# Gate matmuls of a decoder trunk: merged [high | low] products, weight sums on another queue, loads a block ahead

## The chip, the cores and the metric

The kernel runs on one core of a Trainium2 chip. The metric is the device time of one execution in microseconds (us), as the median of three runs. Engines are called PE (TensorE), ACT (ScalarE), DVE (VectorE), POOL (GpSimd) and SP (SyncE, which here issues nearly all transfers).

## The reference

One layer of a hybrid decoder trunk for 512 tokens, D = 2048, float32. The input is normalised and modulated (h), one projection w_in gives all branches, and the gates of the two branches come from the same projection:

```
p = h @ w_in[l]
cv, cg, cz, q, k, v, az, m_conv, m_attn = jnp.split(p, offsets, axis=-1)
y_conv = (silu(layer_norm(conv(cv * sigmoid(cg)))) * silu(cz)) @ w_conv_out
y_attn = (rms_norm(diff_attention(q, k, v)) * (1 - lam_0) * silu(az)) @ w_attn_out
merged = sigmoid(m_conv) * y_conv + sigmoid(m_attn) * y_attn
x = x + gate * rms_norm(merged @ w_o[l], g_post[l])
```

(The conv and attention lines are shortened.) The change concerns the columns cz (1024 wide), m_attn and m_conv (2048 wide each) of the projection. The code's names for the two m parts are ma and mc: the 8 blocks ma and the 8 blocks mc.

## The kernel before

Every large product is made in float32 precision from pairs: a value is split into a high part (a cast, ACT, line 145) and a low part (value minus high, DVE, line 146), and mm3 (lines 165 to 171) issues three matmuls for each 128x128 piece of weights, high·high, high·low and low·high. Weights come as 1 MB pieces through wraw (line 154, three buffers, SP's queue) and are split by wsplit into 128x1024 high and low tiles (wh and wl, three buffers each).

Stages follow one another on TensorE: conv and modulation (0 to 243 us), values, queries, keys and attention heads (to 605), az (559.5 to 664.7, the silu gate of attention; groups az0 to az3 of 256 columns), then the gate stage (664.7 to 1072.5), the attention output (py_ya, to 1159.6), the conv output (py_yc, to 1247) and the last projection (pw).

The gate stage makes 20 blocks of 256 output columns: cz0 to cz3, ma0 to ma7, mc0 to mc7. Each block is one step of a two-by-two Strassen scheme with 7 products instead of 8 (gemm_blocks, line 681). A product is 8 pieces of weights times mm3 on 256 moving columns, 24 matmuls; a block has 168. The weight operands are a11, a12, a22 straight from the loaded pieces, and four sums s1 = a21 + a22, s2 = s1 + a11, s3 = a11 + a21, s4 = s2 + a12 that DVE makes (lines 705, 706, 715, 724). The moving operands are quarters of h (B11, B21, B22, T1) and sums of them (T2, T3, T4), which block_sums makes on DVE and ACT during az, a step at a time (paced). The accumulators z, x and y each take up several products, and DVE joins their intermediate states in ta and tb (lines 711 to 727). The order of the products is z (a11), x (s2), y (s1), x (s3), z (a12), x (a22), y (s4): the second product of a block needs s2.

PE's order in the stage is fixed by the order of the code (ordered). The other engines' orders follow a scheduler that places instructions by its own estimates of readiness, so an instruction can stand behind one that waits. pump advances other work (conv_stats: mean and variance of the conv branch, fetched as cv and stored as cd) by one step after each product. Finished tiles are stored to DRAM by spill (line 433, SP's queue) and read back by fetch (line 438).

The tiles of the gate stage lie in a pool (mq, line 668) that is opened where the pool of the attention stage is closed (front.close(), line 667): the first writer of such a tile waits for the users of the space that was there before.

## Time and profile before

| what | us |
|---|---|
| median of three runs (1434.76 to 1435.95) | 1435.48 |
| the profiled execution | 1436.9 |
| its span in the trace | 1435.1 |
| PE busy in the span | 1397.3 (97%) |
| DVE busy | 1080.9 (75%) |
| ACT busy | 522.1 (36%) |
| gate stage, 664.7 to 1072.5 | 407.8 |

The span is what the trace covers; some 1.8 us of the execution lie around it. PE is busy nearly throughout, so what PE does one after the other makes the time, except at the ends and where it waits.

### The profile page before, as it was taken

Reading aid. Unit: us, or ns where it says so; the run is one execution under the profiler, and the core shown is the slowest. Engines: PE = TensorE matmul, PEld = TensorE weight load, DVE = VectorE, ACT = ScalarE, POOL = GpSimd, SP = SyncE. Lnnn points to the kernel's source line nnn. Section 1 sums busy time; section 2 is a strip of 40 time slices with the busy share of each in tenths; the row PEclk is TensorE's granted clock in tenths of the full one; section 3 lists DMA queues with packets and bytes.
Section 4 is the critical chain, followed back from the end, with each engine's and each line's share of the span. In section 5 each row is a group of like instructions: output and inputs, shape, how many; then the busy total and the mean of one; then the engine's idle time right before and its main releaser. Section 6 shows DMA issues by size and latency. Waiting matters only on the chain.

```text
span 1435.1 us, 20362 instructions
## 1 busy us (share of the span) xinstructions
PE 1397.3 (97%) x7999; PEld 1189.5 (83%) x7999; DVE 1080.9 (75%) x1750; ACT 522.1 (36%) x839; POOL 1.8 (0%) x8
## 2 busy tenths in 40 slices
...
GB/s 301 288 280 304 237 123 92 125 121 59 117 67 96 103 67 84 86 111 142 224 128 192 198 170 174 172 140 121 134 233 350 280 243 181 88 107 231 190 147 147
DMA packets 178338, 238.62 MB, mean 166 GB/s; under 512 B 8689, under 2 KB 119618, under 8 KB 177346
## 3 DMA queue, kind: packets, MB, share of 16 engines
...
HBM read 210.02 MB, written 27.26 MB: 165 GB/s over the span
## 4 chain that ended last, share of the span: by engine, by line
PE 90%; DVE 5%; DMA 2%; ACT 1%; issue 1%; SPq 0%; DVEq 0%; ACTq 0%
PE pw L167 12%; PE pc L167 11%; PE py_ya L167 6%; PE py_yc L167 6%; PE pv L167 6%; PE pg_az L167 5%; PE pg_q L167 5%; PE pg_k L167 5%; PE x_ma L167 5%; PE x_mc L167 4%; PE z_ma L167 3%; PE y_ma L167 3%; PE y_mc L167 3%; PE z_mc L167 3%; PE x_cz L167 2%; PE y_cz L167 2%
## 5 line engine op out<-in xcount | busy, mean ns | idle before, releaser
L500 DVE SCALAR_TENSOR_TENSOR cacc<-u,cw,cacc 128x511 f32<-128x511 f32 (+14 forms) x240 | 164.4, 728 | 0.0
L167 PE MATMUL pc<-hp,wh_c 128*128 128x512 f32 x512 | 159.9, 397 | 3.0 <-DVE part L369 1.2
L167 PE MATMUL pw<-wh_o,mgs 128*128 128x512 f32 x448 | 140.6, 393 | 0.0
L167 PEld LDWEIGHTS pc<-hp,wh_c 128*128 128x128 f32 x512 | 95.6, 190 | 29.0 <-issue 2.7
L167 PE MATMUL pc<-hp,wl_c 128*128 128x512 f32 x256 | 99.0, 396 | 2.1 <-DVE wl_c L146 2.1
L167 PEld LDWEIGHTS pw<-wh_o,mgs 128*128 128x128 f32 x448 | 84.1, 188 | 18.9 <-ACT fsq L932 0.7
L167 PE MATMUL pw<-wl_o,mgs 128*128 128x512 f32 x224 | 87.2, 389 | 0.0
L369 DVE TENSOR_TENSOR part<-pc,part 128x512 f32<-128x512 f32 x96 | 64.7, 687 | 25.3 <-PE pc L167 25.0
L167 PE MATMUL pv<-wh_v,hp 128*128 128x512 f32 x256 | 82.8, 397 | 0.9 <-DVE part L369 0.9
L167 PE MATMUL pg_q<-hp,wh_q 128*128 128x512 f32 x256 | 82.7, 398 | 0.0
L167 PE MATMUL pg_az<-hp,wh_az 128*128 128x512 f32 x256 | 81.5, 395 | 0.0
L167 PE MATMUL pg_k<-hp,wh_k 128*128 128x512 f32 x256 | 80.1, 392 | 0.0
L167 PE MATMUL py_ya<-ya,wh_ya 128*128 128x512 f32 x256 | 78.7, 389 | 0.0
L146 DVE TENSOR_TENSOR wl_o<-wr_o,wh_o 128x1024 fp32r<-128x1024 f32 x28 | 34.2, 1222 | 52.7 <-ACT wh_o L145 52.7
L145 ACT CAST wh_c<-wr_c 128x1024 fp32r<-128x1024 f32 (+1 forms) x36 | 34.2, 955 | 104.0 <-DMA wr_c<-in_w_in_dram 54.9
L889 DVE SCALAR_TENSOR_TENSOR accg<-adag,cact,accg 128x512 f32<-128x512 f32 x60 | 45.1, 751 | 32.2 <-DMA adag<-in_w_ada_dram 31.1
L145 ACT CAST wh_o<-wr_o 128x1024 fp32r<-128x1024 f32 x28 | 29.5, 1052 | 104.5 <-PE pw L167 93.0
L167 PEld LDWEIGHTS pc<-hp,wl_c 128*128 128x128 f32 x256 | 48.5, 190 | 14.1 <-DVE wl_c L146 3.3
L167 PEld LDWEIGHTS pv<-wh_v,hp 128*128 128x128 f32 x256 | 47.8, 188 | 14.3 <-issue 4.5
L167 PEld LDWEIGHTS pg_az<-hp,wh_az 128*128 128x128 f32 x256 | 47.7, 188 | 12.0 <-issue 2.7
L167 PEld LDWEIGHTS pg_q<-hp,wh_q 128*128 128x128 f32 x256 | 47.2, 188 | 12.4 <-issue 2.8
L167 PEld LDWEIGHTS py_ya<-ya,wh_ya 128*128 128x128 f32 x256 | 48.0, 188 | 9.9
...
## 6 DMA issues: line engine op xcount, KB each, us to landing
ada<-in_w_ada_dram SPq DMA_DIRECT2D x128, 256.0 KB, 5.4
wr_ma<-in_w_in_dram SPq DMA_DIRECT2D x16, 1024.0 KB
wr_mc<-in_w_in_dram SPq DMA_DIRECT2D x16, 1024.0 KB, 5.2
adag<-in_w_ada_dram SPq DMA_DIRECT2D x32, 512.0 KB, 5.0
wr_o<-in_w_o_dram SPq DMA_DIRECT2D x16, 1024.0 KB, 5.1
wr_c<-in_w_in_dram SPq DMA_DIRECT2D x28, 512.0 KB, 6.1
wr_v<-in_w_in_dram SPq DMA_DIRECT2D x8, 1024.0 KB, 5.1
wr_q<-in_w_in_dram SPq DMA_DIRECT2D x8, 1024.0 KB, 5.0
```

Source lines behind the costliest of these rows:

```text
L145: nc.scalar.copy(hi, src)
L146: i = nc.vector.tensor_tensor(lo, src, hi.bitcast(F32), op=ALU.subtract)
L167: mm = nc.tensor.matmul(ps, a[p], b[q], start=start and i == 0, stop=stop and i == 2, skip_group_check=more)
L369: nc.vector.tensor_tensor(part[i], ps[f], part[i], op=ALU.add)
L500: paced(nc.vector.scalar_tensor_tensor(cvo[t][:, s:], u[t][:, :S - s], wj, cvo[t][:, s:], op0=ALU.mult, op1=ALU.add))
L889: nc.vector.scalar_tensor_tensor(acc, raw[:, k, :], s1, acc, op0=ALU.mult, op1=ALU.add)
```

## The change

The pair of a moving operand is kept in one tile (hp, halves_of), high part and low part side by side. Where a product is wide, the high weights multiply [high | low] as one matmul of 512 columns into a full bank, and the low weights multiply the high part (256 columns) into its first half: two matmuls instead of three. DVE adds the second half afterwards (comb, and the added lines behind the copies of z). z and y products are wide in every block, x products in mc alone.

s1 is made by two transfers on POOL's queue, a copy and an accumulating one; in mc, s3 too (an accumulating transfer into the loaded piece). Loads go a block ahead (block_load, next_load), o and az of the ma blocks too, and these are now split in place. All stores of the stage go to ACT's queue. conv_stats advances at every other product. block_sums splits T2, T3 and T4 apart, 256 columns each. Temporary tiles are 10 instead of 12, s1 has two buffers and s2 one.

```diff
 NTEMP = 14
-NTEMP2 = 12
+NTEMP2 = 10
...
+                hp[k] = pair_of(f"hp_{k}")
+                h[k] = hi, lo = hp[k][:, 0, :], hp[k][:, 1, :]
...
+    def spill(key, g, queue=nc.sync):
         scratch[key] = dram.tile([P, S], F32, name=f"scratch_{key}")
-        nc.sync.dma_start(out=scratch[key], in_=g)
+        queue.dma_start(out=scratch[key], in_=g)
...
-    T23, T4 = [None] * KH, [None] * KH
+    T2, T3, T4 = [None] * KH, [None] * KH, [None] * KH
     t1s = [temp(f"t1_{i}") for i in range(KH // 2)]
+
+    def halves_of(src, name):
+
+        g = page(name, F32R)
+        split(src, g[:, :H2], g[:, H2:], pace=True)
+        return g.rearrange("p (a n) -> p a n", a=2)
...
-            hi, lo = page(f"t23h_{k}", F32R), page(f"t23l_{k}", F32R)
-            split(t23, hi, lo, pace=True)
-            T23[k] = (hi, lo)
+            T2[k] = halves_of(t23[:, :H2], f"t2_{k}")
+            T3[k] = halves_of(t23[:, H2:], f"t3_{k}")
             yield
-            if k % 2:
-                hi, lo = page(f"t4h_{k}", F32R), page(f"t4l_{k}", F32R)
-                split(t4, hi, lo, pace=True)
-                for i in range(2):
-                    T4[k - 1 + i] = (hi[:, i * H2:(i + 1) * H2], lo[:, i * H2:(i + 1) * H2])
-                yield
+            T4[k] = halves_of(t4[:, half], f"t4_{k}")
+            yield
...
+    B11 = [g[:, :, :H2] for g in hp[:KH]]
+    T1 = [g[:, :, H2:] for g in hp[:KH]]
+    B21 = [g[:, :, :H2] for g in hp[KH:]]
+    B22 = [g[:, :, H2:] for g in hp[KH:]]
...
+    blocks, done = {}, [0]
+
+    def block_load(src, c0, name):
+
+        s1 = mp.tile([P, KH, P], F32, tag="s1", bufs=2, name=f"s1_{name}")
+        v = src.rearrange("(t p) n -> p t n", p=P)
+        nc.gpsimd.dma_start(out=s1, in_=v[:, :KH, c0 + P:c0 + 2 * P])
+        nc.gpsimd.dma_start(out=s1, in_=v[:, KH:, c0 + P:c0 + 2 * P], accum_op=ALU.add)
         r1 = wraw(src, 0, KH, c0, 256, f"{name}_1")
-        r2 = wraw(src, KH, KH, c0, 256, f"{name}_2")
-        a11, a21 = r1[:, :, :P], r1[:, :, P:]
+        if name[:2] == "mc":
+            nc.gpsimd.dma_start(out=r1[:, :, P:], in_=v[:, :KH, c0:c0 + P], accum_op=ALU.add)
+        blocks[name] = [s1, r1]
+        yield
+        blocks[name].append(wraw(src, KH, KH, c0, 256, f"{name}_2"))
...
+        s1, r1, r2 = blocks.pop(name)
+        a11, s3 = r1[:, :, :P], r1[:, :, P:]
         a12, a22 = r2[:, :, :P], r2[:, :, P:]
-
-        def tsum(i):
-            return mp.tile([P, KH, P], F32, tag="ws", bufs=2, name=f"ws_{name}_{i}")
-
-        def prod(ps, w, b, first):
+        s2 = mp.tile([P, KH, P], F32, tag="s2", bufs=1, name=f"s2_{name}")
+        xwide = name[:2] == "mc"
+
+        def prod(ps, w, b, first, wide=True):
 
             hi, lo = w
+            psv = ps.rearrange("p (a n) -> p a n", a=2)
             for k in range(KH):
-                mm3(ps[:, :H2], (hi[:, k, :], lo[:, k, :]), b[k], first and k == 0, k == KH - 1, not first, ordered)
-            pump(rate[0])
+                if wide:
+                    ordered(nc.tensor.matmul(psv, hi[:, k, :], b[k], start=first and k == 0, stop=False,
+                                             skip_group_check=True))
+                    ordered(nc.tensor.matmul(ps[:, :H2], lo[:, k, :], b[k][:, 0, :], start=False, stop=k == KH - 1,
+                                             skip_group_check=True))
+                else:
+                    mm3(ps[:, :H2], (hi[:, k, :], lo[:, k, :]), (b[k][:, 0, :], b[k][:, 1, :]), first and k == 0,
+                        k == KH - 1, not first, ordered)
+            done[0] += 1
+            if done[0] % 2:
+                pump(rate[0])
+
+        def comb(out, ps, a, op0, op1, wide=True):
+
+            nc.vector.tensor_tensor(out, ps[:, :H2], a, op=op0)
+            if wide:
+                nc.vector.tensor_tensor(out, ps[:, H2:], out, op=op1)
 
         z, xx, y = [gbank(f"{n}_{name}", tag) for n, tag in (("z", "g"), ("x", "s"), ("y", "g"))]
-        s1, s2 = tsum(1), tsum(2)
         ta, tb = temp(f"ta_{name}"), temp(f"tb_{name}")
-        q1, u2 = ta[:, :H2], ta[:, H2:]
+        q1, u2 = tb[:, :H2], ta[:, H2:]
         w11 = wsplit(a11, f"{name}_a11")
-        nc.vector.tensor_tensor(s1, a21, a22, op=ALU.add)
+        prod(z, w11, B11, True)
         nc.vector.tensor_tensor(s2, s1, a11, op=ALU.add)
-        prod(z, w11, B11, True)
         nc.scalar.copy(q1, z[:, :H2])
+        nc.vector.tensor_tensor(q1, z[:, H2:], q1, op=ALU.add)
         ws2 = wsplit(s2, f"{name}_s2")
-        prod(xx, ws2, T2, True)
+        prod(xx, ws2, T2, True, xwide)
+
         nc.vector.tensor_tensor(u2, q1, xx[:, :H2], op=ALU.subtract)
+        if xwide:
+            nc.vector.tensor_tensor(u2, u2, xx[:, H2:], op=ALU.subtract)
         ws1 = wsplit(s1, f"{name}_s1")
         prod(y, ws1, T1, True)
-        nc.vector.tensor_tensor(tb[:, H2:], q1, y[:, :H2], op=ALU.add)
-        nc.vector.tensor_tensor(a21, a11, a21, op=ALU.add)
-        ws3 = wsplit(a21, f"{name}_s3")
-        prod(xx, ws3, T3, False)
-        nc.vector.tensor_tensor(tb[:, H2:], xx[:, :H2], tb[:, H2:], op=ALU.subtract)
+        comb(tb[:, H2:], y, q1, ALU.add, ALU.add)
+        if name[:2] != "mc":
+            nc.vector.tensor_tensor(s3, a11, s3, op=ALU.add)
+        ws3 = wsplit(s3, f"{name}_s3")
+        prod(xx, ws3, T3, False, xwide)
+        next(loads[0], None)
+        comb(tb[:, H2:], xx, tb[:, H2:], ALU.subtract, ALU.add, xwide)
         w12 = wsplit(a12, f"{name}_a12")
         prod(z, w12, B21, False)
+        nc.scalar.copy(ta[:, :H2], z[:, :H2])
+        nc.vector.tensor_tensor(ta[:, :H2], z[:, H2:], ta[:, :H2], op=ALU.add)
         w22 = wsplit(a22, f"{name}_a22")
-        prod(xx, w22, T4, False)
-        nc.vector.tensor_tensor(tb[:, :H2], xx[:, :H2], q1, op=ALU.subtract)
+        prod(xx, w22, T4, False, xwide)
+        comb(q1, xx, q1, ALU.subtract, ALU.add, xwide)
         nc.vector.tensor_tensor(s2, s2, a12, op=ALU.add)
         ws4 = wsplit(s2, f"{name}_s4")
         prod(y, ws4, B22, False)
-        nc.vector.tensor_tensor(u2, u2, y[:, :H2], op=ALU.add)
-        return z, ta, tb
-
-    def silu2(i, z, ta, tb):
+        comb(u2, y, u2, ALU.add, ALU.add)
+        return ta, tb
...
+    todo = [(C_CZ + j * 256, f"cz{j}") for j in range(4)]
+    todo += [(c0 + j * 256, f"{name}{j}") for c0, name in ((C_MA, "ma"), (C_MC, "mc")) for j in range(8)]
+    todo = deque(todo)
+
+    loads = [block_load(w_in[0], *todo.popleft())]
+    for _ in range(2):
+        next(loads[0], None)
...
+    def next_load():
+
+        loads[0] = block_load(w_in[0], *todo.popleft()) if todo else iter(())
+        next(loads[0], None)
+
     for pair in range(4):
-        gs = silu2(pair, *gemm_blocks(w_in[0], C_CZ + pair * 256, f"cz{pair}"))
+        next_load()
+        gs = silu2(pair, *gemm_blocks(f"cz{pair}"))
         for f in range(2):
-            spill(f"cz{2 * pair + f}", gs[f])
+            spill(f"cz{2 * pair + f}", gs[f], nc.scalar)
     for c0, name in ((C_MA, "ma"), (C_MC, "mc")):
         for j in range(8):
-            z, ta, tb = gemm_blocks(w_in[0], c0 + j * 256, f"{name}{j}")
-            g0, g1 = temp(f"{name}0_{j}"), temp(f"{name}1_{j}")
-            nc.scalar.activation(g0[:, :H2], z[:, :H2], AF.Tanh, scale=0.5)
-            nc.scalar.activation(g0[:, H2:], ta[:, H2:], AF.Tanh, scale=0.5)
-            nc.scalar.activation(g1, tb, AF.Tanh, scale=0.5)
-            spill(f"{name}{2 * j}", g0)
-            spill(f"{name}{2 * j + 1}", g1)
+            next_load()
             if name == "ma":
                 o, az = temp(f"o_{j}"), temp(f"az_{j}")
                 fetch(f"o{j}", o)
                 fetch(f"az{j}", az)
+            ta, tb = gemm_blocks(f"{name}{j}")
+            g0, g1 = temp(f"{name}0_{j}"), temp(f"{name}1_{j}")
+            nc.scalar.activation(g0, ta, AF.Tanh, scale=0.5)
+            nc.scalar.activation(g1, tb, AF.Tanh, scale=0.5)
+            spill(f"{name}{2 * j}", g0, nc.scalar)
+            spill(f"{name}{2 * j + 1}", g1, nc.scalar)
+            if name == "ma":
                 nc.vector.tensor_tensor(o, o, az, op=ALU.mult)
-                hi, lo = temp(f"oh_{j}", F32R), temp(f"ol_{j}", F32R)
-                split(o, hi, lo)
-                spill(f"yah{j}", hi.bitcast(F32))
-                spill(f"yal{j}", lo.bitcast(F32))
+                split(o, az.bitcast(F32R), o.bitcast(F32R))
+                spill(f"yah{j}", az, nc.scalar)
+                spill(f"yal{j}", o, nc.scalar)
```

The first place is the border between az and the first gate block, on DVE. Names: wl_az, hp and t4l are splits of az weights, of t1 and of the block sums; ws_cz (after: s_cz) are weight sums, wl_cz_s their low parts. Before:

```order
L146 TENSOR_TENSOR t4l_5523<-t_6_5443,t4h_5522 128x512
L146 TENSOR_TENSOR wl_az_12_5551<-wr_az_8_5510,wh_az_12_5550 128x1024
L146 TENSOR_TENSOR wl_cz_a_5624<-wr_cz_1_5612,wh_cz_a_5623 128x1024
L705 TENSOR_TENSOR ws_cz_1_5619<-wr_cz_1_5612,wr_cz_2_5614 128x1024
L706 TENSOR_TENSOR ws_cz_2_5620<-ws_cz_1_5619,wr_cz_1_5612 128x1024
L715 TENSOR_TENSOR wr_cz_1_5612<-wr_cz_1_5612 128x8x128
L146 TENSOR_TENSOR wl_cz_s_5657<-ws_cz_2_5620,wh_cz_s_5656 128x1024
L724 TENSOR_TENSOR ws_cz_2_5620<-ws_cz_2_5620,wr_cz_2_5614 128x1024
```

After, from the last block sum's split (t, 128x256):

```order
L146 TENSOR_TENSOR t_7_5575<-t_6_5489,t_7_5575 128x256
L748 TENSOR_TENSOR wr_cz_1_5646<-wr_cz_1_5646 128x8x128
L658 SCALAR_TENSOR_TENSOR sz_5618<-sz_5618,pg_az_0_5432 128x512
L658 SCALAR_TENSOR_TENSOR sz_5623<-sz_5623,pg_az_1_5433 128x512
L737 TENSOR_TENSOR tb_cz_5653<-z_cz_5649,tb_cz_5653 128x256
L735 TENSOR_TENSOR s_cz_5648<-s_cz_5636,wr_cz_1_5639 128x1024
L146 TENSOR_TENSOR wl_cz_s_5680<-s_cz_5648,wh_cz_s_5679 128x1024
L146 TENSOR_TENSOR wl_cz_s_5709<-s_cz_5636,wh_cz_s_5708 128x1024
L146 TENSOR_TENSOR wl_cz_s_5732<-wr_cz_1_5639,wh_cz_s_5731 128x1024
```

The last split of block sums stood ahead of the az and cz splits and three rows ahead of the first weight sum; now those splits come earlier, and it is the last one before the gate stage's own work. s2 (L735) stands behind a sum for the next block (L748), the two sz and the first add on z (L737), and DVE no longer makes s1.

POOL issues s1's transfers in this order (L687 the copy, L688 the accumulating one), where before it issued none:

```order
L687 DMA s_cz_5636<-in_w_in_dram 128x8x128
L687 DMA s_cz_5643<-in_w_in_dram 128x8x128
L688 DMA s_cz_5636<-in_w_in_dram 128x8x128
L688 DMA s_cz_5643<-in_w_in_dram 128x8x128
L687 DMA s_cz_5846<-in_w_in_dram 128x8x128
L688 DMA s_cz_5846<-in_w_in_dram 128x8x128
```

The copies of the first two blocks go out together, then their second halves; from there each block's pair follows the other.

The second place is the end of the stage on SP's queue, around the second weights of the attention output (the wr_ya row here). Before:

```order
L155 DMA wr_ya_10376<-in_w_attn_out_dram 128x8x256
L435 DMA scratch_mc_10122<-mc_6_10116 128x512
L435 DMA scratch_mc_10120<-mc_6_10115 128x512
L883 DMA adag_0_11085<-in_w_ada_dram 128x2x512
L155 DMA wr_ya_10469<-in_w_attn_out_dram 128x8x256
L438 DMA ya_10350<-scratch_yah_6865 128x512
L438 DMA ya_10350<-scratch_yal_6867 128x512
```

After:

```order
L438 DMA ya_9667<-scratch_yal_8228 128x512
L438 DMA mg_9730<-scratch_ma_6706 128x512
L438 DMA mg_9730<-scratch_ma_6708 128x512
L438 DMA cd_9745<-scratch_cd_6582 128x512
L438 DMA cd_9747<-scratch_cd_6696 128x512
L438 DMA cd_9749<-scratch_cd_6837 128x512
L438 DMA tz_9751<-scratch_cz_5842 128x512
L155 DMA wr_ya_9765<-in_w_attn_out_dram 128x8x256
L438 DMA mg_9823<-scratch_ma_6923 128x512
```

The second wr_ya went from ahead of all fetches of ya (16) to behind them, behind the first mg pair, the last three cd and the first tz.

The third place is DVE right behind that, at the low parts of these weights (wl_ya) and the addition of the first attention output (mg). Before:

```order
L727 TENSOR_TENSOR ta_mc_10133<-ta_mc_10133,y_mc_10130 128x256
L146 TENSOR_TENSOR wl_ya_0_10472<-wr_ya_10469,wh_ya_0_10471 128x1024
L146 TENSOR_TENSOR wl_ya_4_10500<-wr_ya_10469,wh_ya_4_10499 128x1024
L851 TENSOR_TENSOR cd_10443<-cd_10443,crs 128x512
L851 TENSOR_TENSOR cd_10445<-cd_10445,crs 128x512
L851 TENSOR_TENSOR cd_10447<-cd_10447,crs 128x512
L851 TENSOR_TENSOR cd_10449<-cd_10449,crs 128x512
L851 TENSOR_TENSOR cd_10451<-cd_10451,crs 128x512
L905 SCALAR_TENSOR_TENSOR mg_10434<-mg_10434,py_ya_0_10374 128x512
L905 SCALAR_TENSOR_TENSOR mg_10434<-mg_10434,py_ya_1_10375 128x512
```

After:

```order
L898 TENSOR_TENSOR cd_9749<-cd_9749,crs 128x512
L903 SCALAR_TENSOR_TENSOR cd_9735<-cth_9752,cd_9735 128x512
L905 TENSOR_TENSOR cd_9735<-cd_9735,tz_9751 128x512
L151 SCALAR_TENSOR_TENSOR ycl_9760<-cd_9735,ych_9759 128x512
L952 SCALAR_TENSOR_TENSOR mg_9730<-mg_9730,py_ya_0_9670 128x512
L146 TENSOR_TENSOR wl_ya_0_9768<-wr_ya_9765,wh_ya_0_9767 128x1024
L952 SCALAR_TENSOR_TENSOR mg_9730<-mg_9730,py_ya_1_9671 128x512
L146 TENSOR_TENSOR wl_ya_4_9796<-wr_ya_9765,wh_ya_4_9795 128x1024
```

The two low parts stood ahead of the two mg additions, with sums of cd between; now each stands behind one of them.

## Rows read from the trace of the kernel before

**Rows 1.** Gate stage: length, busy us by engine, PEclk, DMA share, GB/s.

```profile
664.70:747.00 82.30, 82.30 (x683) 81.82 (x682) 73.92 (x105) 40.50 (x54) 0.00 (x0) 1.00 0.53 180
747.00:909.80 162.80, 162.47 (x1354) 162.28 (x1354) 131.18 (x149) 74.93 (x96) 0.00 (x0) 1.00 0.55 181
909.80:1072.50 162.70, 161.57 (x1347) 161.39 (x1346) 117.89 (x127) 71.29 (x89) 0.00 (x0) 1.00 0.46 155
```

**Rows 2.** Waits of TensorE in the gate stage: us in total, times, longest.

```profile
PE x_mc L167 <- DVE tb_mc L718: 1.1, 1, 1.1
```

**Rows 3.** Timeline, TensorE, end of az, first block: start, us, operation.

```profile
664.01 0.62 PE L167 MATMUL pg_az<-hp,wh_az 128*128 128x512 f32 x2
...
664.69 0.40 PE L167 MATMUL z_cz<-hp,wh_cz_a 128*128 128x256 f32 x2
...
667.56 1.02 PE L750 MATMUL pmean<-csum,ones 128*128 128x512 f32 x2
668.02 0.68 PE L167 MATMUL x_cz<-t23h,wh_cz_s 128*128 128x256 f32 x1
```

**Rows 4.** VectorE and ScalarE groups, gate stage: busy us, mean ns, idle.

```profile
L705 DVE TENSOR_TENSOR ws_ma<-wr_ma,wr_ma 128x1024 f32<-128x1024 f32 x8 | 9.8, 1220 | 0.3 <-DMA wr_ma<-in_w_in_dram 0.3
...
L723 DVE TENSOR_TENSOR tb_ma<-x_ma,ta_ma 128x256 f32<-128x256 f32 x8 | 3.4, 424 | 1.5 <-PE x_ma L167 1.3
...
L145 ACT CAST wh_ma_s<-ws_ma 128x1024 fp32r<-128x1024 f32 x24 | 25.2, 1050 | 37.8 <-PE x_ma L167 23.8 <-PE y_ma L167 9.2 <-PE x_cz L167 1.6
```

**Rows 5.** Timeline, VectorE, the last az group.

```profile
643.08 0.69 DVE L657 SCALAR_TENSOR_TENSOR sz<-sz,pg_az 128x512 f32<-128x512 f32 x1 [1.21 <-ACT sz L656]
...
646.07 0.42 DVE L146 TENSOR_TENSOR hp<-t,hp 128x256 fp32r<-128x256 f32 x1
646.40 0.42 DVE L628 TENSOR_TENSOR hf<-hf,hf 128x256 f32<-128x256 f32 x1
646.74 1.22 DVE L146 TENSOR_TENSOR wl_az<-wr_az,wh_az 128x1024 fp32r<-128x1024 f32 x1
647.87 0.42 DVE L630 TENSOR_TENSOR hf<-hf,t 128x256 f32<-128x256 f32 x1
...
656.04 0.69 DVE L146 TENSOR_TENSOR t4l<-t,t4h 128x512 fp32r<-128x512 f32 x1 [0.18 <-ACT t4h L145]
...
660.17 1.23 DVE L706 TENSOR_TENSOR ws_cz<-ws_cz,wr_cz 128x1024 f32<-128x1024 f32 x1
```

**Rows 6.** Transfers from 560 to 1160: count, KB each, median us to landing.

```profile
wr_cz<-in_w_in_dram SPq DMA_DIRECT2D x8, 1024.0 KB, 5.4
wr_ya<-in_w_attn_out_dram SPq DMA_DIRECT2D x8, 1024.0 KB, 10.0
adag<-in_w_ada_dram SPq DMA_DIRECT2D x11, 512.0 KB, 4.9
```

**Rows 7.** Granted clock (PEclk) of three stretches, and TensorE in two.

```profile
20.00:25.00 5.00, 3.75 (x27) 3.01 (x28) 3.34 (x11) 0.99 (x2) 0.00 (x0) 1.00 1.15 331
138.40:145.30 6.90, 6.90 (x24) 6.03 (x24) 3.03 (x7) 2.67 (x5) 0.00 (x0) 0.51 0.64 219
1428.60:1435.00 6.40, 0.00 (x0) 0.00 (x0) 2.15 (x4) 0.00 (x0) 0.00 (x0) 0.51 0.56 216
...
21.07 1.19 PE L243 MATMUL prs<-diag,ones 128*128 128x128 f32 x4 [4.26 <-DVE diag L242]
...
141.02 0.77 PE L167 MATMUL pc<-hp,wl_c 128*128 128x512 f32 x1
```

**Rows 8.** Timeline, SyncE's queue and VectorE at the end of the stage.

```profile
1057.64 0.38 SPq L155 DMA_DIRECT2D wr_ya<-in_w_attn_out_dram  x1
...
1073.66 1.23 DVE L146 TENSOR_TENSOR wl_ya<-wr_ya,wh_ya 128x1024 fp32r<-128x1024 f32 x1 [0.58 <-ACT wh_ya L145]
...
1084.29 1.28 DVE L905 SCALAR_TENSOR_TENSOR mg<-mg,py_ya 128x512 f32<-128x512 f32 x2
```

**Rows 9.** Busy us, share and instructions of each engine, from the page.

```profile
PE 1397.3 (97%) x7999; PEld 1189.5 (83%) x7999; DVE 1080.9 (75%) x1750; ACT 522.1 (36%) x839; POOL 1.8 (0%) x8
```

More of the change, by code (lines that the diff above doesn't have):

```diff
@@ L171, in mm3 @@
         return mm
-    h = [None] * KT
+    h, hp = [None] * KT, [None] * KT
     part = [None] * 16
@@ L335, in ada @@
                 nc.scalar.activation(hf, xn[k], AF.Identity, scale=scl[:, b:b + 1], bias=sh[:, b:b + 1])
-                g = pair_of(f"hp_{k}")
-                h[k] = hi, lo = g[:, 0, :], g[:, 1, :]
+                hp[k] = pair_of(f"hp_{k}")
+                h[k] = hi, lo = hp[k][:, 0, :], hp[k][:, 1, :]
                 split(hf, hi, lo)
@@ L431, in hybrid_trunk @@
     scratch = {}
-    def spill(key, g):
+    def spill(key, g, queue=nc.sync):
         scratch[key] = dram.tile([P, S], F32, name=f"scratch_{key}")
-        nc.sync.dma_start(out=scratch[key], in_=g)
+        queue.dma_start(out=scratch[key], in_=g)
     def fetch(key, g):
@@ L658, in hybrid_trunk @@
             spill(f"az{hd}", g)
-    B11 = [(hi[:, :H2], lo[:, :H2]) for hi, lo in h[:KH]]
-    T1 = [(hi[:, H2:], lo[:, H2:]) for hi, lo in h[:KH]]
-    T2 = [(hi[:, :H2], lo[:, :H2]) for hi, lo in T23]
-    T3 = [(hi[:, H2:], lo[:, H2:]) for hi, lo in T23]
-    B21 = [(hi[:, :H2], lo[:, :H2]) for hi, lo in h[KH:]]
-    B22 = [(hi[:, H2:], lo[:, H2:]) for hi, lo in h[KH:]]
+    B11 = [g[:, :, :H2] for g in hp[:KH]]
+    T1 = [g[:, :, H2:] for g in hp[:KH]]
+    B21 = [g[:, :, :H2] for g in hp[KH:]]
+    B22 = [g[:, :, H2:] for g in hp[KH:]]
     front.close()
@@ L688, in gemm_blocks @@
+    def gemm_blocks(name):
+        s1, r1, r2 = blocks.pop(name)
+        a11, s3 = r1[:, :, :P], r1[:, :, P:]
         a12, a22 = r2[:, :, :P], r2[:, :, P:]
-        def tsum(i):
-            return mp.tile([P, KH, P], F32, tag="ws", bufs=2, name=f"ws_{name}_{i}")
-        def prod(ps, w, b, first):
+        s2 = mp.tile([P, KH, P], F32, tag="s2", bufs=1, name=f"s2_{name}")
+        xwide = name[:2] == "mc"
+        def prod(ps, w, b, first, wide=True):
             hi, lo = w
+            psv = ps.rearrange("p (a n) -> p a n", a=2)
```

15 lines of the change are left out of this document (6 added, 9 removed).

## The prediction

> **What bounds the kernel now.** I read the stretches first. In the gate stage TensorE is busy 82.30 of 82.30, 162.47 of 162.80 and 161.57 of 162.70 us, VectorE 90, 81 and 72%, the DMA engines about half [rows 1]. So the stage's time is the number of matmuls times the distance from one start to the next, and the only wait of weight in it is one of 1.1 us [rows 2]. A gain must come from that distance; anything added counts only where TensorE then waits. The distance is in the timeline [rows 3]: three 512-column matmuls go from 664.01 to 664.69, 0.2267 us each; the 24 256-column ones of z_cz go from 664.69 to 667.56, 0.1196 each. The columns alone would make one exactly twice the other; so each matmul carries something of its own beyond its columns, and fewer, wider ones save it.
>
> Then I read what stands on both sides of the gate stage, since the order listings show that the change rewrites its entry and its exit. Before it, VectorE works nearly without a break, and the block sums end at 656.73, so that the first weight sums are made long before TensorE begins x_cz at 668.02 [rows 3, 5]. That slack is what the change uses up.
>
> **The merged matmuls** remove 832 matmuls: 4 of 7 products in 12 blocks (32 triples each) and 7 of 7 in 8 blocks (56 each), 384 + 448. A triple is 3 × 0.1196 = 0.3588 us now, and 0.2267 + 0.1196 = 0.3463 after: 12.5 ns less, 832 times: **−10.4 us**, all on the path. Bounds: nothing, if reading a [high | low] pair in two pieces costs what it saves, to −11.
>
> That a matmul has a fixed part shows in [rows 3]: 12.5 ns per matmul saved. The Trainium skill, "TensorE: Matmul & The Clock Gate", section "Wait — 56ns, not 53.3ns?", puts the fixed cost of a matmul at about 2.5 ns. By that the merge would give an estimated 2 us, and the sum below would be 8 us later; the trace disagrees here.
>
> **Weight sums on GpSimd's queue.** VectorE loses 20 sums (28 with mc's third) of 1.22 us and gains the second-half adds of 0.42 [rows 4]. A ma block is then 10 × 1.22 + 2 × 0.69 + 9 × 0.42 = 17.4 us, against 16.4 now (131.18 / 8, [rows 1]), in a block of 19.7: not the bound, with less room. In steady state the two or three GpSimd transfers of a block are a block ahead and cost nothing while copy and accumulate together take under 19.7 us. The transfers use DMA time, which is half free [rows 1].
>
> What one such transfer takes no row shows: GpSimd has 8 instructions and no transfer [rows 9]. Nearest rows: 4.9 us to landing for 512 KB (adag), 10.0 for the slowest 1 MB group [rows 6]. I take 4.9 for each, copy and accumulate, since the bytes are the same.
>
> **The entry** is the main cost. The first copy waits for all users of the pool that is closed there; the last is the VectorE split of t4_7. When does it end? Now 27 VectorE operations go from 643.08 (the first of the two sz) to the last block sum's end at 656.73, 13.65 us [rows 5]. After, 41 stand between the same two: 13 more of 256 columns (0.335 each, 646.07 to 646.40 to 646.74), 2 more of 1024 (1.13, 646.74 to 647.87), one fewer of 512 (0.61). 13.65 + 4.36 + 2.26 − 0.61 = 19.66: the end is at 662.7. Copy until 667.6, accumulate until 672.5, s2 1.22, its cast 1.05, its low part 1.22 [rows 4], hand-overs 0.3: the low weights of x_cz are there at 676.3.
>
> TensorE comes earlier. In the last az group the low part of the second weights stands behind 12 operations, 4 × 0.61 + 8 × 0.335 = 5.1 us and some 0.3 of waits after 643.08, so it ends at 649.7, and not at 647.96 [rows 5]; TensorE wants it at about 648.8 (the second quarter of the 96 matmuls that end at 664.69 begins 72 × 0.2267 earlier, at 648.4; its third matmul reads the low part): **+0.9** (0 to 1.5). Then z from 665.6 for 8 × 0.347 = 2.8, pmean 0.46, two matmuls: 669.1. The wait for x_cz is 676.3 − 669.1 = **+7.2**.
>
> Its bounds: were the sums there at once, VectorE's order still sets q1 (after z's last matmul, 668.4, a copy and an add of 0.42 each) ahead of s2: 669.3 + 1.22 + 1.05 + 1.22 + 0.3 = 673.1, a wait of 4.0. With 10.0 for each transfer: 662.7 + 20 + 3.8 = 686.5, a wait of 17.4.
>
> **The clock.** Pauses of up to 4.3 us in the first 25 us were followed by a granted clock of 1.00, but 3.9 us after the last matmul it is at 0.51 (1.2 GHz) [rows 7]. After the only-narrow matmuls ahead of 141.02 it is at 0.51 too, and dense 512-column work from 141.02 ran at half speed until 145.3: 4.2 us of work that was worth 2.1. A wait of 7.2 us should cost the same: **+2.1** (0, if the wait stays near 4; 3.4 if all of such a 6.9 us stretch is dense).
>
> **The exit.** Let G be the end of the gate stage, now 1072.45. Two things move. On VectorE the low part of ya1's first weights now stands behind mg's addition of py_ya0; before it stood ahead (1073.66 against 1084.29, [rows 8]). py_ya0's first bank is done at G + 10.2 (45 of 48 matmuls), the addition takes 0.64, the low part 1.22: G + 12.1, and TensorE wants it at G + 11.3: 0.8. And SP issues ya1's weights after the ya fetches, mg and cd, not ahead of them (1057.64, [rows 8]): mg waits for the last product (G − 2.8), six issues of about 0.5 follow, and the slot may wait for mg's landing: issue at G + 0.3 to G + 5, landing after 5.4 to 10.0 [rows 6], so at G + 5.7 to G + 15; the middle is G + 10.4, cast and low part G + 12.7. **+1.4** (0.8 to 6).
>
> **The rest.** The old wait in mc went with a late weight load behind queued stores; loads are now a block ahead and stores elsewhere: **−1.1** [rows 2]. 64 stores on ScalarE's queue are hidden by ScalarE's free half (74.93 of 162.80) and by casts that wait for TensorE anyway (23.8 us, [rows 1, 4]); without that cover they hold the next cast and become a rival, below. o and az a block ahead, two temps fewer, statistics pumped every other product: zero, covered by the same slack; a few tenths otherwise.
>
> Sum against the profiled 1436.9: −10.4 − 1.1 + 0.9 + 7.2 + 2.1 + 1.4 = **+0.1**, so 1437.0. That execution lies 1.4 above the median of 1435.48, so 1435.6 on that footing. A measurement here tells 0.2%, 2.9 us, from no change.
>
> **Rivals.** *Short entry.* GpSimd's pair of transfers takes under about 6.6 us, so VectorE's order, not the transfer, sets s2: the wait is 4.0 and the clock stays. 1435.6 − 3.2 − 2.1 = 1430.3. For it: stores of 256 KB and loads in quiet stretches are short, and the start's pauses of 4.3 us cost no clock [rows 7]. Against it: an accumulate reads and writes, and a 1 MB load of cz1 runs beside it. The Trainium skill, "DMA: Bandwidth & Descriptors", section "Anatomy of one DMA — SWDGE (gpsimd) path", gives 2.0 us plus bytes over 436 GB/s, an estimated 3.2 us for 512 KB: by it the pair ends at 669.1 and this rival holds. No row here shows it.
>
> *Slow accumulate (the slower side).* Copy and accumulate take 10.0 us each, as the ya weights do [rows 6]. Place: the first block, where nothing is ahead; wait 17.4: +10.2, so 1445.8. It decides from some 6.3 us each (2.8 us over the forecast); above 9.8 each every block waits for it as well, and the time goes past 1450. For it: 512-byte runs, read and write. Against it: half the DMA engines are free.
>
> *Lost cover.* In the 12 cz and ma blocks VectorE is at 88% and more, and ScalarE issues stores in order among the casts; a late cast holds TensorE by about 0.5 us per block, half of the one wait that [rows 2] shows: +6, 1441.6. Against it: cz ran at 90% VectorE without a wait [rows 1].
>
> *The merge does nothing.* The two-piece read takes 0.239 per wide matmul, twice 0.1196: no gain, 1446.0.
>
> **How the numbers follow.** The forecast has 0.48, with an own range of 1431 to 1441; of it 0.32 lies within 0.2%, 0.08 below and 0.08 above. Short entry 0.28, slow accumulate 0.12, lost cover 0.07, no merge 0.05. Faster: 0.28 + 0.08 = 0.36; same 0.32; slower 0.12 + 0.07 + 0.05 + 0.08 = 0.32. The range reaches from the short entry with its exit at the low bound and the az wait at zero (1430.3 − 0.6 − 0.9, about 1428.5) to the slow accumulate, 1446; above it lies half of that case and some of the others, below it a tenth at most.
>
> **What would show it.** Right: wide matmuls 0.227 apart and blocks of 19.7 and 19.4 us; x_cz held by s2 for some 7 us, the accumulate's landing ahead of it; a stretch of half clock behind that; a wait of 1 to 3 us at the second ya block; nothing of weight between. The short entry shows as s2 right behind q1 and a clock of 1.00; the slow accumulate as a wait of over 12 us. Wrong would be waits in every block, or a gate stage, without its entry, not 10 us shorter.

## The result and the profile after

| | before | after |
|---|---|---|
| median (4 runs each) | 1435.72 us (1434.76 to 1436.87) | 1475.69 us (1473.75 to 1476.71) |
| span of the profiled execution | 1435.1 | 1474.9 |

The change makes the kernel slower: ratio 1.0278, 95% interval 1.0266 to 1.029. The forecast was 1435.6, its range ended at 1446.0. (The kernel before, run again beside every experiment below, took 1435.4 to 1435.7 each time, so the times of different runs may be subtracted.) By stretches of the two traces (first matmul of a block to the first of the next):

| stretch | before | after | difference | forecast |
|---|---|---|---|---|
| up to z_cz0 | 664.69 | 665.96 | +1.3 (0.7 of it ahead of az) | +0.9 |
| cz0 | 21.00 | 31.68 | +10.7 | +8.9 |
| cz1 to ma7, 11 blocks | 224.13 | 252.12 | **+28.0** | **-4.4** |
| mc, 8 blocks | 162.62 | 160.66 | -2.0 | -6.7 |
| after the stage | 362.65 | 364.5 | +1.9 | +1.4 |

(The forecast's terms by place: cz0 has the entry and the clock, and each of the twelve cz and ma blocks 32 x 12.5 ns, each mc block 56 x 12.5 ns of the merge.) So the two ends came out near their prices, mc gained 4.7 us less than forecast, and the miss lies in the eleven blocks between. The same windows as [rows 1] for after begin at 664.7 (length, busy us by engine, PEclk, DMA share, GB/s):

```profile
664.70:760.00 95.30, 79.88 (x508) 71.78 (x507) 66.41 (x87) 37.95 (x48) 14.09 (x12) 0.93 0.73 185
760.00:920.00 160.00, 145.63 (x949) 132.35 (x948) 118.28 (x169) 67.82 (x87) 15.66 (x13) 0.97 0.76 211
920.00:1080.00 160.00, 160.00 (x942) 140.55 (x941) 124.53 (x170) 73.35 (x91) 31.14 (x23) 1.00 0.97 228
```

TensorE is idle for 15.4 and 14.4 us of the first two and never in the third (mostly mc). In the first two windows VectorE is *less* busy (70 and 74%) than in the first two of [rows 1] (90 and 81%), so it was not overloaded: it stood still. Transfers went from about half of the DMA engines' time to three quarters and more. The page shows what was added (first line as [rows 9], then the queues: packets, MB, share of 16 engines):

```profile
PE 1405.3 (95%) x7167; PEld 1152.2 (78%) x7167; DVE 1085.8 (74%) x1834; ACT 527.3 (36%) x851; POOL 63.5 (4%) x56
...
q1 hardware_dynamic: 169026, 220.53, 45.3%
q0 software_dynamic: 32000, 25.17, 10.8%
```

TensorE's waits, as [rows 2] (us in total, times, longest), and VectorE's from 690 to 950:

```profile
PE x_cz L167 <- ACT wh_cz_s L145: 8.3, 1, 8.3
PE x_ma L167 <- DVE wl_ma_s L146: 6.8, 4, 2.3
PE z_ma L715 <- DVE wl_ma_a L146: 3.5, 1, 3.5
PE x_ma L167 <- DVE ta_ma L741: 2.3, 4, 0.7
```
```profile
DVE wr_ma L748 <- DMA wr_ma<-in_w_in_dram: 29.2, 8, 5.6
DVE cv L800 <- DMA cv<-scratch_cv: 11.3, 4, 3.9
...
DVE wr_cz L748 <- DMA wr_cz<-in_w_in_dram: 5.1, 2, 2.7
```

The first is the entry. The others are spread over the later cz and ma blocks, and they are late low parts and late additions, as VectorE stands 29.2 + 5.1 us at L748, the sum s3 in place of the loaded a21. In the eleven blocks TensorE is idle for 21.0 us, and it works 13.7 us at a granted clock of 0.50, which is worth another 6.8; two of the four stretches at that clock (columns as in [rows 1]):

```profile
723.40:726.60 3.20, 3.20 (x12) 2.71 (x12) 3.17 (x5) 0.05 (x1) 0.00 (x0) 0.50 0.02 5
819.00:822.20 3.20, 3.20 (x16) 3.10 (x15) 2.81 (x4) 1.15 (x2) 0.91 (x1) 0.50 0.00 0
```

One wait at L748 in full, on VectorE (start, us, operation, idle before it and releaser), TensorE, and from the chain of waits of the same stretch:

```profile
803.39 1.22 DVE L146 TENSOR_TENSOR wl_ma_a<-wr_ma,wh_ma_a 128x1024 fp32r<-128x1024 f32 x1
...
808.99 0.42 DVE L756 TENSOR_TENSOR ta_ma<-z_ma,ta_ma 128x256 f32<-128x256 f32 x1
814.93 1.23 DVE L748 TENSOR_TENSOR wr_ma<-wr_ma 128x1024 f32<-128x1024 f32 x1 [5.52 <-DMA wr_ma<-in_w_in_dram]
816.07 0.42 DVE L726 TENSOR_TENSOR tb_ma<-x_ma,tb_ma 128x256 f32<-128x256 f32 x1
816.41 1.21 DVE L146 TENSOR_TENSOR wl_ma_s<-s_ma,wh_ma_s 128x1024 fp32r<-128x1024 f32 x1
```
```profile
817.67 0.39 PE L167 MATMUL x_ma<-t,wl_ma_s 128*128 128x256 f32 x1 [2.35 <-DVE wl_ma_s L146]
```
```profile
804.64 10.27 DMA wr_ma<-in_w_in_dram
```

The low part that ends at 804.6 frees a weight buffer; the load into it starts at 804.64 and lands 10.27 us later. VectorE reaches the sum on that piece after 4.8 us of other work and stands for 5.5. The low part of s2 that TensorE wants now is behind it. The sum itself was in no hurry. In VectorE's order, s2 (L735) and the first low part of a block stand beside s3 of the block *after* it (here the first ma block; the trace has these four from 764.42 to 769.18):

```
L735 TENSOR_TENSOR s_ma_6500<-s_ma_6275,wr_ma_1_6278 128x1024
L146 TENSOR_TENSOR wl_ma_a_6507<-wr_ma_1_6278,wh_ma_a_6506 128x1024
L756 TENSOR_TENSOR ta_cz_6284<-z_cz_6281,ta_cz_6284 128x256
L748 TENSOR_TENSOR wr_ma_1_6494<-wr_ma_1_6494 128x8x128
```

The block that uses the sum made at 814.93 begins at 837.00, and s3 is its fourth product. In mc, where a transfer makes s3, no block but the last waits.

The theory at this point: the merged kernel loses its time to one VectorE instruction ordered right where its load is still under way; a longer landing makes it worse. Rivals: the crowd of transfers slows whatever waits for a load (traffic), or the merged matmuls bring their own waits.

### The profile page after: what moved, and what is told of

It is laid out like the page before. It is cut to its first block, busy times and chain, and to the rows that moved or that the text cites. A ratio compares the mean times of both kernels' runs of the same rounds, so it can differ in the third digit from the quotient of the medians.

```text
span 1474.9 us, 18868 instructions
## 1 busy us (share of the span) xinstructions
PE 1405.3 (95%) x7167; PEld 1152.2 (78%) x7167; DVE 1085.8 (74%) x1834; ACT 527.3 (36%) x851; POOL 63.5 (4%) x56
## 3 DMA queue, kind: packets, MB, share of 16 engines
q1 hardware_dynamic: 169026, 220.53, 45.3%
q0 software_dynamic: 32000, 25.17, 10.8%
## 5 line engine op out<-in xcount | busy, mean ns | idle before, releaser
L167 PEld LDWEIGHTS py_ya<-ya,wh_ya 128*128 128x128 f32 x256 | 47.9, 188 | 11.4 <-ACT wh_ya L145 1.6
```

What stands on the lines that cost most here:

```text
L167: mm = nc.tensor.matmul(ps, a[p], b[q], start=start and i == 0, stop=stop and i == 2, skip_group_check=more)
```

## The experiments

**The sum's place and the sum itself.** First, an order token that keeps s3 behind the block's first y addition.

```diff
-        comb(tb[:, H2:], y, q1, ALU.add, ALU.add)
+        comb(tb[:, H2:], y, q1, ALU.add, ALU.add, stamp=True)
-            nc.vector.tensor_tensor(s3, a11, s3, op=ALU.add)
+            i3 = nc.vector.tensor_tensor(s3, a11, s3, op=ALU.add)
+            tc.stamp_issue_order_token(i3.ins, "sums")
```

> The changed kernel with one thing fixed: on VectorE, the sum s3 of a block is kept behind that block's first addition on y, by an order token on the two; nothing else in the code. Theory 1 (order): s3 of a later block stands early in VectorE's order, in place in the freshly loaded weights, so VectorE waits for that load's landing (29.2 us over the 8 ma blocks) and all behind it is late; with s3 at its place the cz1 to ma7 blocks fall from 20 to 25 us to some 19.9 each: 31 us less, about 1445 us. The loads still land some 9 us after issue. Theory 2 (contention): GpSimd's copy and accumulate crowd the DMA engines, loads are late whatever the order: at most 5 us less, above 1470. Theory 3 (too much work on VectorE and ScalarE in these blocks): no change, 1475.

1513.92 us, ratio 1.0553 (1.0537 to 1.0569): a miss, since the token went too far. y's end is where x(s3) begins, so its weights now start late (TensorE's two longest waits):

```profile
PE x_ma L167 <- ACT wh_ma_s L145: 20.2, 8, 2.7
PE x_cz L167 <- ACT wh_cz_s L145: 19.1, 5, 8.1
```

With the token behind q1 (L737) instead, s3 keeps a product's time ahead of its use:

> The changed kernel with one order fixed: on VectorE the sum s3 of a block is kept behind that block's first addition on z (q1), one product earlier than in the first trial of an order, where the sum stood behind an addition that waits for y's product, and the next product (x with s3) wants its low weights at once, so that each block gained a wait of 3.8 us. Loads, transfers and all else are those of the changed kernel. Theory 1 (an early s3 waits for a load that has just been issued): with the sum at this place the cz1 to ma7 blocks are 19.9 us, some 31 us less than the changed kernel, about 1445, while the weight loads still take 7 to 9 us to land. Theory 2 (the crowd of transfers alone): above 1470. The entry's wait of some 8 us stays under both.

1457.01 us, ratio 1.0157 (1.0141 to 1.0172). Neither expectation came: it lies between 1445 and 1470. Waits at s3 are gone from VectorE's list, cz1 to ma7 fall from 252.12 to 234.74, and the weights land in 5.8 us (median) instead of 9.1, where both theories had them stay slow. The order alone, with the same bytes, gives back 18.7 of the 40 us. What stays is the entry (TensorE waits 8.3 us there) and waits of the same kind at other places, the longest where VectorE stands 5.0 us at a fetched cd.

Next, the sum itself: made by an accumulating transfer in all blocks, and left out in cz and ma (there the product takes plain a21).

```diff
-        if name[:2] == "mc":
+        if True:      # e2_accum: s3 by transfer in all blocks
             nc.gpsimd.dma_start(out=r1[:, :, P:], in_=v[:, :KH, c0:c0 + P], accum_op=ALU.add)
...
-        if name[:2] != "mc":      # e2_accum and e12_no_s3
-            nc.vector.tensor_tensor(s3, a11, s3, op=ALU.add)
```

> The changed kernel, with s3 made by an accumulating transfer on GpSimd's queue in all blocks, as it already is in mc; VectorE's s3 sums go (12 of 1.22 us). Theory 1: the sum that waited is gone, blocks cz1 to ma7 fall to some 19.9 us, about 1445 us, or a little less at the entry. Theory 2: 12 more transfers of 512 KB on engines that are crowded already: loads land later than 9 us and the time goes up, 1476 to 1490. Theory 3: 12 x 1.22 us of VectorE work less, some 1.2 us per block at most: 1462.

> The changed kernel with the third sum left out in the cz and ma blocks (that product then takes the plain a21 as weights, so this part of the computation is changed); all transfers stay. If VectorE's wait at this sum is the cause, cz1 to ma7 go from 252 to 222 to 227 us, the wait at the entry stays at 8, and the time is 1447 to 1452. If the crowd of transfers holds VectorE at some other place anyway (statistics, low parts), the blocks stay above 235 and the time above 1458.

1451.77 us (1.0122, 1.0103 to 1.0142) and 1447.57 us (1.009, 1.0073 to 1.0107), the first between two of its expectations (1445 and 1462), the second within its first. Most blocks run at 19.93 us, and cz1 to ma7 take 226.37 and 226.27. In e2_accum, which has 12 transfers more, TensorE waits 10.5 us at the entry. TensorE's waits without the sum, the entry first:

```profile
PE x_cz L167 <- ACT wh_cz_s L145: 7.9, 1, 7.9
PE x_ma L167 <- DVE wl_ma_s L146: 2.7, 2, 1.5
```

One VectorE instruction per block, 12 x 1.22 us of work, was worth 28 us.

**Traffic.** All of GpSimd's transfers away, every sum on VectorE:

```diff
-        nc.gpsimd.dma_start(out=s1, in_=v[:, :KH, c0 + P:c0 + 2 * P])
-        nc.gpsimd.dma_start(out=s1, in_=v[:, KH:, c0 + P:c0 + 2 * P], accum_op=ALU.add)
...
+        nc.vector.tensor_tensor(s1, r1[:, :, P:], a22, op=ALU.add)
         nc.vector.tensor_tensor(s2, s1, a11, op=ALU.add)
```

> The changed kernel without any transfer on GpSimd's queue: s1 and s3 of all blocks are sums on VectorE again; loads a block ahead, merged matmuls, stores on ScalarE's queue stay. It also takes away the entry's wait for the accumulate (8.7 us, and 1.5 us of half clock behind it). Theory 1: sums still stand ahead of later needs and wait for loads, but loads land in 5 to 6 us and not 9: about half of the 31 us stays, 1450. Theory 2: with the crowd gone everything lost goes: 1475.7 - 10 - 31, about 1435. Theory 3: 28 more sums of 1.22 us on VectorE: 1480 or more.

1438.27 us (1.0018, 1.0004 to 1.0031), near the second expectation. VectorE has 20 s1 and 8 more s3 of 1.22 us to do, and hardly anything waits: blocks of 19.93 (20.0 in mc), weights land in 5.4. Only mc7 loses 4.5 us. The loads a block ahead, the merged matmuls and the stores on ScalarE's queue are all in this kernel, so none of them is the cause. So the sums are harmless where loads are quick (cz1 to ma7 take 221.8), and the transfers nearly harmless where s3 is left out (226.27, 4.5 more). To take the two apart, e8_dve_wf (below, 1428.45 us) got the copy and the accumulating transfer again, into a tile that nobody reads:

```diff
-NTEMP2 = 10
+NTEMP2 = 8
+        idle = mp.tile([P, KH, P], F32, tag="idle", bufs=1, name=f"idle_{name}")
+        nc.gpsimd.dma_start(out=idle, in_=v[:, :KH, c0 + P:c0 + 2 * P])
+        nc.gpsimd.dma_start(out=idle, in_=v[:, KH:, c0 + P:c0 + 2 * P], accum_op=ALU.add)
```

> The kernel of e8_dve_wf, with the change's copy and accumulating transfer of each block on GpSimd's queue again, but into a tile that nobody reads; VectorE, ScalarE and TensorE have the same instructions in the same order through the gate stage (two temporary tiles fewer make room for the tile). Only the traffic is added. If the transfers lengthen the weight loads enough to make VectorE wait, the landing of the weights goes from 5.5 to 7 to 9 us, waits on them come back in cz1 to ma7, and the time is 1440 to 1455. If traffic alone does nothing and the waits come from the order of VectorE in the changed kernel, it stays at 1428.5 within 3 us.

1464.9 us (1.0199, 1.0172 to 1.0225): 36.4 us more than the same kernel without the idle transfers, above both expectations. But 11.2 of it fell at the very end: from the last matmul to the end of the span it is 21.5 us here and 10.3 to 10.5 in every other kernel. There VectorE's last additions come late (VectorE's last row, e8_dve_wf and e10_crowd; TensorE's last matmul ends at 1412.96 and 1446.45):

```profile
1416.29 2.74 DVE L1032 SCALAR_TENSOR_TENSOR xr<-og,fr_y,xr 128x512 f32<-128x512 f32 x4
```
```profile
1460.49 2.74 DVE L1032 SCALAR_TENSOR_TENSOR xr<-og,fr_y,xr 128x512 f32<-128x512 f32 x4 [3.56 <-DMA xr<-in_x_dram]
```

GpSimd transfers nothing there; the likely cause is the two temporary tiles that this kernel lacks, which was not tested apart, there or in the stage. Without the tail the transfers cost some 25 us, and 1464.9 less 11.2 is 1453.7, within the first expectation; cz1 to ma7 go from 220.34 to 247.13.

Weight loads from 690 to 950 (count, KB, median us to landing), e8_dve_wf, e10_crowd, after, e12_no_s3:

```profile
wr_ma<-in_w_in_dram SPq DMA_DIRECT2D x16, 1024.0 KB, 5.5
```
```profile
wr_ma<-in_w_in_dram SPq DMA_DIRECT2D x16, 1024.0 KB, 9.4
```
```profile
wr_ma<-in_w_in_dram SPq DMA_DIRECT2D x16, 1024.0 KB, 9.1
```
```profile
wr_ma<-in_w_in_dram SPq DMA_DIRECT2D x16, 1024.0 KB, 7.2
```

and the waits that came with the idle transfers (VectorE, then TensorE):

```profile
DVE s_ma L737 <- DMA wr_ma<-in_w_in_dram: 12.0, 4, 4.7
DVE s_mc L737 <- DMA wr_mc<-in_w_in_dram: 5.9, 1, 5.9
DVE cv L803 <- DMA cv<-scratch_cv: 5.3, 2, 4.8
```
```profile
PE x_ma L167 <- DVE tb_ma L727: 13.3, 5, 4.3
PE x_cz L167 <- DVE tb_cz L727: 4.6, 2, 4.2
```

VectorE's order through the stage is the same in the traces of e8_dve_wf and e10_crowd. That settles the theory against its first form: the order decides *where* VectorE stands, the traffic makes the landing long enough to stand for. In cz1 to ma7 the sums without the traffic cost nothing that shows (e3_dvesums), the traffic without s3 4.5 us (e12_no_s3); together they cost 30.3 (after against e3_dvesums) and 26.8 (e10_crowd against e8_dve_wf).

The same bytes do not always lengthen a load, as the 5.8 us of e1c_order show. The packets in the traces of after, e1c_order and e6c_best (below) show what differs: loads of ma weights from 690 to 950 during which GpSimd's queue moved at most 0.15 MB landed in 5.5 to 6.0 us (8 loads), those that met 0.45 MB or more took 6.5 to 12.7 us (9 loads). In after all six whose landing the trace has met 0.45 to 0.63 MB. So the order also sets which transfers meet.

**The entry**, priced by letting VectorE make s1 in the first block alone (the e3_dvesums lines under `if name == "cz0":`):

> The changed kernel with the first block's s1 made by VectorE, and all else as it is: it prices the entry alone. The wait of x_cz at the entry was 8.3 us with 1.5 us of half clock behind it; the order of VectorE then sets s2, which the forecast put at a wait of 4.0. So 4 to 10 us are gained: 1466 to 1472. If the entry's pause is made up later, or moves to a following block, the time stays at 1475.7.

1466.35 us (1.0222, 1.02 to 1.0244): 9.3 us gained. cz0 goes from 31.68 to 20.78; of these 10.9 us, 2.4 come back as waits in cz1 to ma7 and 1.5 in mc7, and z_cz0 begins 2.5 us earlier, by scatter ahead of az.

**The merge.** Alone, on the kernel before (pair tiles, two matmuls for three, added second halves; loads, sums and stores as before):

> The kernel before with the merged matmuls alone: pair tiles, second-half additions, separate splits of T2, T3, T4. Weight sums on VectorE, loads, stores and statistics as before. By the measured distances 832 triples of 360.0 us/1000 become 353.3: 5.6 us less, if VectorE with 1.0 us more work per block (some 93% busy in cz and ma) holds nothing up: 1430. If VectorE becomes the bound in the cz and ma blocks: waits of 0.5 to 1 us each, 1436 to 1442.

1496.0 us (1.0425, 1.041 to 1.0439), the opposite sign. The schedule again: ma2 to mc0 take 26.9 to 27.4 us each, as the second-half addition of z (here L724) stands behind a low part whose cast waits for a buffer that TensorE's running product must free.

```profile
858.86 1.23 DVE L146 TENSOR_TENSOR wl_ma_a<-wr_ma,wh_ma_a 128x1024 fp32r<-128x1024 f32 x1 [0.99 <-ACT wh_ma_a L145]
...
860.61 0.42 DVE L724 TENSOR_TENSOR tb_ma<-z_ma,tb_ma 128x256 f32<-128x256 f32 x1
...
862.07 0.41 DVE L728 TENSOR_TENSOR ta_ma<-tb_ma,x_ma 128x256 f32<-128x256 f32 x1
```
```profile
PE x_ma L167 <- DVE ta_ma L728: 32.8, 7, 4.8
```

So this run says nothing on the matmuls' own price. In after, where no block of mc0 to mc6 waits, a pair takes 353.3 ns (236.6 behind a wide one, 116.7 behind a narrow one) against 360.0 for three narrow ones. Issuing the eight wide matmuls of a product first and the eight narrow ones behind them:

```diff
+            if wide:
+                for k in range(KH):
+                    ordered(nc.tensor.matmul(psv, hi[:, k, :], b[k], ...))
+                for k in range(KH):
+                    ordered(nc.tensor.matmul(ps[:, :H2], lo[:, k, :], b[k][:, 0, :], ...))
```

> The changed kernel, with the wide products issued as 8 matmuls of 512 columns, then 8 of 256, instead of alternating. Alternating, a start to the next is 236.6 ns behind a wide and 116.7 behind a narrow one, 353.3 the pair, where 346.3 was forecast from 226.7 and 119.6 in runs of one width. If it is the alternation that costs: 346.3, 7 ns for 832 pairs, 5.8 us less; and since the low weights are wanted 1.6 us later, part of the waits on low parts goes as well: 1465 to 1470. If a wide matmul that is read in two pieces simply takes 236.6: no change in the distances, 1473 to 1476.

1464.14 us (1.0219, 1.0189 to 1.025); 349.6 ns per pair, between the two expectations, and mc blocks of 19.55 instead of 19.78. The pairs are worth 3.1 of the 11.6 us; the rest are waits that fell otherwise. The merge without disturbance is the difference of the next two.

**Put together.** All sums on VectorE, wide matmuls first; then the same kernel with narrow triples and without the added second halves:

> The changed kernel with all weight sums on VectorE (no transfer on GpSimd's queue) and, in wide products, 8 wide matmuls ahead of 8 narrow ones. That without the second part took 1438.3, with mc blocks of 20.0 us and a last one of 24.5. Wide first: 349.6 ns a pair (measured in the trial with GpSimd's transfers) and not 353.3: 832 x 3.7 = 3.1 us less, and the low weights are wanted 1.6 us later, so small waits in mc (0.2 us a block) and part of the last block's 4.5 us go: 1430 to 1435. If VectorE is the bound in mc: 1437.

> The kernel of e8_dve_wf with narrow triples in all products and without the 832 merged pairs and the adds of the second half: it prices the merge where no block waits. If a merged pair, wide matmuls first, takes 349.6 ns and a narrow triple 360.0 (both measured in blocks without waits), 832 x 10.4 ns = 8.7 us come back: 1428.5 + 8.7 = 1437.1. If the forecast's step was right (12.5 ns each), 1438.9. If the merge is worth nothing there either, 1428 to 1430, and then the gain of e8_dve_wf comes from the loads and stores alone.

1428.45 us (0.995, 0.9938 to 0.9963), faster than both kernels and 1.6 below its expectation, and 1437.08 us (1.001, 1.0 to 1.002). In the gate stage of the first TensorE has no wait beyond 0.2 us; most blocks take 19.81 (cz, ma) and 19.55 (mc). The merge is worth 8.6 us, 10.4 ns in each of 832 places, as expected. The second kernel is 1.7 us above the kernel before, at the edge of its interval: what is left of the change there, the loads a block ahead and the stores on ScalarE's queue among it, gains nothing that can be measured.

The last one keeps GpSimd's transfers and mends what the other runs showed: first s1 on VectorE, s3 behind q1, wide first.

> The changed kernel with three repairs: s1 of the first block as a sum on VectorE, s3 kept behind q1 in VectorE's order, wide matmuls ahead of narrow ones. If the three losses are what the trace says, all blocks are 19.8 (cz, ma) and 19.55 us (mc), the entry's wait is gone: 12 x 19.8 + 8 x 19.55 + 2.8 for the statistics' matmuls = 396.8 us from z of cz0 to the attention output, against 407.8 before; the az stage some 1.5 us longer, the exit some 1.5: 1427 to 1430. If the crowd of transfers itself costs the blocks anything, 1440 or more.

1439.82 us (1.003, 1.0019 to 1.0042), at the edge of its second expectation (1440 or more), and 11.4 us above e8_dve_wf, where GpSimd transfers nothing. The entry is clean, but VectorE still stands for late fetches, this one for 4.9 us:

```profile
DVE cd L905 <- DMA cd<-scratch_cd: 4.9, 1, 4.9
```

## Why the prediction was wrong

**The step that failed** is in the weight sums: "In steady state the two or three GpSimd transfers of a block are a block ahead and cost nothing". The sums themselves were ready: in the ma blocks of after a copy lands in 4.7 to 5.9 us, its accumulating transfer in 10.4 to 15.3 (4.9 was taken for each), and still no s2 but the first waits for s1. The cost lay elsewhere. The step asked whether the *sums* would be ready, and counted free DMA time; it did not ask what else waits for a load. [rows 6] had the price: 5.4 to 10.0 us for 1 MB. Set against the 4.8 us of VectorE work between the load's release and L748 (which only the trace of after gives), that is 0.6 to 5.2 us of standstill per block, 7 to 57 us over eleven. The order around L748 was shown ahead of the prediction at the entry (s2 behind "a sum for the next block"), and was priced neither there nor in the blocks. The rival *lost cover* had the right blocks, but took its 0.5 us from the one wait of [rows 2], which is no row on a load; without waits (e3_dvesums) the eleven blocks take 221.8, so the waits, with the half clock among them, cost 30.3 us, 2.75 a block. Of these 25.9 go when s3 is left out (226.27, e12_no_s3). The statistics' fetches, put at zero, are likely part of the rest: from 690 to 950 VectorE stands 11.3 us at fetched cv. "The transfers use DMA time, which is half free" was wrong in effect: the share went from 0.58 (e8_dve_wf) to 0.89 (e10_crowd) from 690 to 920, and the landing from 5.5 to 9.4.

**The entry** was right in mechanism and place. On VectorE, GpSimd and TensorE:

```profile
669.37 0.42 DVE L737 TENSOR_TENSOR tb_cz<-z_cz,tb_cz 128x256 f32<-128x256 f32 x1 [1.90 <-ACT tb_cz L736]
675.77 1.23 DVE L735 TENSOR_TENSOR s_cz<-s_cz,wr_cz 128x1024 f32<-128x1024 f32 x1 [5.97 <-DMA s_cz<-in_w_in_dram]
```
```profile
663.87 1.96 POOL L687 DMA_DIRECT2D s_cz<-in_w_in_dram  x2 [660.96 <-DVE t L146]
669.39 3.17 POOL L688 DMA_DIRECT2D s_cz<-in_w_in_dram  x2 [3.56 <-DMA s_cz<-in_w_in_dram]
```
```profile
678.12 0.80 PE L167 MATMUL x_cz<-t,wh_cz_s 128*128 128x256 f32 x2 [8.33 <-ACT wh_cz_s L145]
...
681.68 0.63 PE L167 MATMUL x_cz<-t,wh_cz_s 128*128 128x256 f32 x2
682.32 0.41 PE L167 MATMUL x_cz<-t,wh_cz_s 128*128 128x256 f32 x2
```

The copy starts at 663.87 (forecast: from 662.7), takes 5.5 us, the accumulating one 6.4, where 4.9 was taken for each from an adag load of the same bytes. The wait is 8.3 instead of 7.2. Half speed (granted clock 0.50; 0.64 us per triple instead of 0.36) lasts from 678.1 to 682.3: five triples, 1.4 us instead of 2.1. That the clock would fall was right, as [rows 7] let expect; that it would fall again behind the waits of later blocks (13.7 us at half clock) was not priced. The Trainium skill, "DMA: Bandwidth & Descriptors", section "Anatomy of one DMA — SWDGE (gpsimd) path", gave an estimated 3.2 us for 512 KB; here, beside other transfers, the trace disagrees with 5.5 and 6.4, and *short entry* fell with it. Its bound of 4.0 us stays untested: with s1 on VectorE (e5_entry) the scheduler orders the sums anew, and the first x_cz does not wait at all.

**The merge**, -10.4, had the right kind and was mis-sized: 12.5 ns per place came from long runs of one width in [rows 3]. Alternating widths gave 6.7 in after (832 x 6.7 = 5.6 us), runs of eight 10.4 (8.6 us, e8_dve_wf against e9_nomerge). The old wait in mc (-1.1) went as forecast: mc0 to mc6 have none in after.

**The exit** (+1.4) was right in mechanism: ya1's weights were issued 0.6 us after the stage's end at 1110.4, and TensorE waited 1.1. The rest of the +1.9 is not resolved. mc7 lost 2.4 us that no step named: its second x product waits for the subtraction of the first one's second half.

```profile
1110.99 0.38 SPq L155 DMA_DIRECT2D wr_ya<-in_w_attn_out_dram  x1
```
```profile
PE x_mc L713 <- DVE ta_mc L743: 1.5, 1, 1.5
PE py_ya L167 <- ACT wh_ya L145: 1.1, 1, 1.1
```

**az** (+0.9) was too large: TensorE waited 0.2 us there. That +1.3 was measured is luck: 0.7 of it arose ahead of az, where executions scatter (az begins between 556.6 and 560.9 in the kernels here).
